# Last token group of a ConvFFN: 16 of 22 blocks of the down-projection by seven products for eight, their weight sums made in DRAM by accumulating DMAs

## The chip, the cores and the metric

One NeuronCore of one Trainium2 chip runs the program. The metric is the device time of one execution in microseconds (us); three runs of the kernel before gave 2209.5, 2211.93 and 2210.5 us, a median of 2210.5 us. Durations and waits come from one further execution that the hardware profiler recorded.

## The reference

One layer of a hybrid encoder on 2112 tokens (2048 of a prompt, 64 of a sample), in float32. An attention-like mixer comes first and is not touched by the change. What follows it, per token, with 1024 channels and 2816 hidden units:

```python
h2 = rmsnorm(x, g2) * (1 + sc2) + sh2
up = h2 @ w_up                                   # 1024 -> 2 * 2816
upp = concat([conv_buf, up], 1)                  # two earlier rows
conv = b_conv + sum(w_conv[j] * upp[:, j:j + T] for j in range(3))
a, g = split(conv, 2, -1)
x = x + gt2 * ((silu(g) * a) @ w_down)           # 2816 -> 1024
y = rmsnorm(x, g_final)
```

The outputs are y and the states that a next step needs.

## The kernel before

Channels lie on the 128 partitions and tokens along the free axis. The mixer fills about the first 800 us. The ConvFFN then runs in three token groups of FT = 704 tokens, from 800 to 1262, 1262 to 1727.6 and 1727.6 to 2205.6 us. A group is worked in two halves of FH = 352 tokens, which fit a PSUM bank. The third group holds the prompt's last 640 tokens and the 64 of the sample, so many of its vector operations are cut in two, at 640 of 704 or at 288 of 352.

**fp32 in three passes.** Each operand of a matmul is split into a rounded high part (ACT, `activation` with Copy) and the rest (DVE, a subtraction). A product is high x high, high x low and low x high: three matmuls for each 128x128 weight block and each half of the tokens (`PASSES`).

**Up-projection by seven products.** Hidden units come in 22 blocks of 128; for each block f a `Pair` computes the block of a and the block of g together. Four products of a half of the channels with a half of the tokens for each output, eight in all, are replaced by seven, in Strassen's manner, with sums of weights (`WS1` to `WS4`) and sums of tokens (B21, T2, T3 and so on). `product()` issues 12 matmuls of 352 columns each (L1522), so 84 for a pair. The sums of the weights lie in DRAM as `wsum`. Of the four, WS2 and WS1 are split in group 0 and stored to DRAM as split tiles (`wsplit`, 512 KB, `keep`, L374), which groups 1 and 2 load whole; WS3 and WS4 are loaded unsplit (256 KB) and split again in every group.

**Pair by pair.** While PE runs the products of one pair, DVE and ACT finish the pair before: sums of products into the extended tiles ea and eg (L1530, L1574), the convolution (scale on ACT L1505, taps on DVE L1510), silu (ACT L1616), the gate (DVE L1620) and the split of the result into `av` tiles (ACT L1637, DVE L1645).

**Down-projection.** The 22 blocks of a group are worked in four parts, `PARTS = ((0, 5), (5, 10), (10, 16), (16, 22))`: the pairs of a part, and then their share of the down-projection, whose contraction runs over the blocks of the part. Each of 8 output rows n takes nf blocks x 3 passes x 2 halves of matmuls (L1785) into two PSUM banks; `down_end` (L1800) then adds gt2 times the bank to the x tile of that row. The first NE = 3 rows are begun before the part's last blocks are ready. In the last part of the last group, rows 3 to 7 run in two sections of 448 and 256 tokens (`ENDS`), so that the final norm and the stores of the first section run under the second one; the weights of these rows stay in SBUF.

**Weights.** All weights are one list (`stream`) in the order in which PE needs them. `pump()` issues loads on SP's queue ahead of their use, into 4 raw tiles (RB, L350) or straight into one of 6 split tiles (WB; whole L355, to be split in place L358), and has ACT (L366) and DVE (L369) split them up to three units ahead. The order of instructions on PE, ACT, DVE and POOL is the order of the code (`manual_schedule`); side work (the next group's normalisation and its data sums, loads, the norm of the group before) is cut into steps, which `tick` and `do` place between the products.

## Time and profile before

| | |
|---|---|
| three runs | 2209.5, 2211.93, 2210.5 us (median 2210.5) |
| the profiled execution: span from the first to the last instruction | 2205.6 us |
| median of the runs less that span | 4.9 us |
| mixer | 0 to about 800 us |
| ConvFFN group 0, 1, 2 | 462, 465.6, 478 us |

A row of the table of windows gives the window, its length, then for PE, PE's weight loads (PEld), DVE, ACT and POOL the busy time and the number of instructions, then PE's granted clock (1.00 is full), the busy share of the DMA engines and the GB/s moved. A row of a group of instructions gives the source line, the engine, the operation, output <- inputs with partitions x elements, the number, and then busy time, mean ns of one, and how long the engine idled just before them and on whom it waited. A row of the page's list of DMA issues ends in the median time from issue to landing. All times are microseconds unless a row says otherwise.

### The profile page before, as it was taken

The page shows a single profiled execution, that of the slowest core. Times are in us where ns is not written, and L with a number is a line of the kernel's source. Part 1 is how long each engine was busy: PE and PEld are TensorE (multiplying, and loading weights), DVE is VectorE, ACT ScalarE, POOL GpSimd, SP SyncE. Part 2 cuts the span into 40 slices and gives each one's busy share as a digit, 9 for nine tenths or more (in the row PEclk, how much of TensorE's full clock was granted, in tenths as well). Part 3 has the DMA queues.
Part 4 walks back from the last instruction along what each step waited for, and adds up shares of the span by engine and source line. Part 5 has one row for each costly group of instructions (what it writes and reads, how often), then busy time and mean ns, then how long its engine had stood idle before and what let it go on. Part 6 is the DMA issues. An engine that isn't in the chain of part 4 may idle for free. (4 is left out here: it accounts for less than half of the span.)

```text
span 2205.6 us, 38165 instructions
## 1 busy us (share of the span) xinstructions
PE 2186.1 (99%) x13804; PEld 2079.2 (94%) x13804; DVE 1568.5 (71%) x2916; ACT 1005.3 (46%) x1993; POOL 203.0 (9%) x481
## 2 busy tenths in 40 slices
PE   8999999999999999999999999999999999999998
PEld 7888888888899999999999999999999999999998
DVE  5887669577765778787958587767667685767474
ACT  4653334235243455554636354545344443445354
POOL 0010000001000100010000210000001210101012
PEclk9999999999999999999999999999999999999999
DMA  9977987997898695767557876565458565353442
GB/s 355 367 242 264 333 275 243 324 324 239 292 323 272 223 310 177 234 205 239 188 173 233 266 245 200 183 214 175 144 169 285 186 190 166 111 173 121 150 148 81
DMA packets 279357, 498.58 MB, mean 226 GB/s; under 512 B 25176, under 2 KB 105432, under 8 KB 279168
## 3 DMA queue, kind: packets, MB, share of 16 engines
q1 hardware_dynamic: 267392, 468.05, 65.0%
q10 hardware_dynamic: 11776, 28.09, 3.4%
q8 instruction: 109, 1.79, 0.3%
q14 instruction: 80, 0.66, 0.1%
HBM read 385.29 MB, written 110.75 MB: 225 GB/s over the span
## 5 line engine op out<-in xcount | busy, mean ns | idle before, releaser
L1522 PE MATMUL mm<-hx,wt 128*128 128x352 f32 x5544 | 885.4, 321 | 1.0 <-DVE ea L1574 0.9
L1522 PEld LDWEIGHTS mm<-hx,wt 128*128 128x128 f32 x5544 | 879.5, 188 | 2.1 <-ACT wt L366 1.5
L1785 PE MATMUL mm<-av,wt 128*128 128x352 f32 (+2 forms) x3168 | 508.6, 321 | 0.4 <-DVE av L1645 0.3
L1785 PEld LDWEIGHTS mm<-av,wt 128*128 128x128 f32 x3168 | 502.6, 188 | 3.0 <-DVE av L1645 0.9
L423 PE MATMUL mm<-hl,wt 128*128 128x512 f32 (+2 forms) x1920 | 395.8, 358 | 1.7 <-DMA wt<-hl_kept 1.7
L366 ACT ACTIVATE wt<-raw 128x512 fp32r<-128x512 f32 (+3 forms) x494 | 274.5, 571 | 249.6 <-PE mm L1785 109.3
L369 DVE TENSOR_TENSOR wt<-raw,wt 128x512 fp32r<-128x512 f32 (+3 forms) x494 | 307.0, 637 | 87.5 <-ACT wt L366 81.4
L423 PEld LDWEIGHTS mm<-hl,wt 128*128 128x128 f32 x1920 | 312.6, 188 | 49.4 <-issue 5.3
L1800 DVE SCALAR_TENSOR_TENSOR x<-mm,MOD,x 128x352 f32<-128x352 f32 (+4 forms) x224 | 106.5, 526 | 128.8 <-PE mm L1785 128.8
L423 PE MATMUL mm<-mx,wt 128*128 128x512 f32 (+1 forms) x960 | 186.8, 353 | 0.0
L423 PEld LDWEIGHTS mm<-mx,wt 128*128 128x128 f32 x960 | 158.8, 188 | 25.4 <-ACT mx L1378 1.1
L1510 DVE SCALAR_TENSOR_TENSOR tg<-eg,V,tg 128x704 f32<-128x704 f32 (+1 forms) x132 | 125.7, 952 | 49.3 <-ACT tg L1505 46.8
L369 DVE TENSOR_TENSOR wt<-wt 128x512 fp32r<-128x512 f32 x176 | 121.8, 692 | 49.4 <-ACT wt L366 49.2
L366 ACT ACTIVATE wt<-wt 128x512 fp32r<-128x512 f32 x176 | 110.2, 626 | 75.1 <-DMA wt<-wsum 62.5
L1510 DVE SCALAR_TENSOR_TENSOR ta<-ea,V,ta 128x704 f32<-128x704 f32 (+1 forms) x132 | 125.6, 952 | 7.8 <-ACT ta L1505 5.4
L1645 DVE TENSOR_TENSOR av<-tg,av 128x704 fp32r<-128x704 f32 (+4 forms) x112 | 62.0, 588 | 43.2 <-ACT av L1637 43.0
L1570 ACT ACTIVATE u<-mm 128x352 f32<-128x352 f32 x66 | 30.6, 464 | 120.3 <-PE mm L1522 81.8
L1616 ACT ACTIVATE tg<-tg 128x704 f32<-128x704 f32 (+1 forms) x66 | 52.3, 793 | 68.9 <-DVE tg L1510 68.9
L203 DVE SCALAR_TENSOR_TENSOR acc<-raw,CA,acc 128x512 f32<-128x512 f32 x84 | 60.5, 744 | 32.1 <-DMA raw<-w_ada 32.1
L1530 DVE TENSOR_TENSOR eg<-mm,u 128x352 f32<-128x352 f32 x154 | 70.1, 467 | 18.4 <-ACT u L1585 11.2
L1114 PE MATMUL mm<-wt,hl 128*128 128x256 f32 (+1 forms) x576 | 70.9, 282 | 0.0
L1114 PEld LDWEIGHTS mm<-wt,hl 128*128 128x128 f32 x576 | 69.3, 188 | 1.0 <-issue 0.6
(299 smaller groups left out, 1951.9 us busy)
## 6 DMA issues: line engine op xcount, KB each, us to landing
wt<-hl_kept SPq DMA_DIRECT2D x108, 512.0 KB, 5.9
raw<-w_up SPq DMA_DIRECT2D x198, 256.0 KB, 3.1
wt<-wsum SPq DMA_DIRECT2D x176, 256.0 KB, 4.0
wt<-wsplit SPq DMA_DIRECT2D x88, 512.0 KB, 3.9
raw<-w_down SPq DMA_DIRECT2D x96, 256.0 KB, 3.9
w<-w_up SPq DMA_DIRECT2D x88, 256.0 KB, 5.4
wsum<-w SPq DMA_DIRECT2D x44, 512.0 KB, 5.7
wsplit<-wt SPq DMA_DIRECT2D x44, 512.0 KB, 5.0
```

The lines of the kernel that those rows point to most:

```text
L203: dve.scalar_tensor_tensor(out=acc[s], in0=w, scalar=CA[:, k, s:s + 1], in1=acc[s], op0=ALU.mult, op1=ALU.add)
L366: act.activation(u.w[:, 0, :u.n], u.raw[:, :u.n], AF.Copy)
L369: dve.tensor_tensor(out=u.w[:, 1, :u.n], in0=u.raw[:, :u.n], in1=u.w[:, 0, :u.n].bitcast(F32), op=ALU.subtract)
L423: pe.matmul(ps[bi][:, :hi - lo], U[:, a, k % 4 * P:(k % 4 + 1) * P], mv[k][:, b, lo:hi], start=(at == 0 and pi == 0), stop=(k == order[-1] ...
L1114: pe.matmul(ps[ti][:n, :cols], h[4 * kh + k4][:, b, lo:lo + n], U[:, a, k4 % 2 * cols:(k4 % 2 + 1) * cols], start=(kh == 0 and k4 == 0 and ...
L1510: dve.scalar_tensor_tensor(out=t[:, :E], in0=ext[:, j:j + E], scalar=wc(j, f), in1=t[:, :E], op0=ALU.mult, op1=ALU.add)
L1522: pe.matmul(ps[:, :FH], U[:, a, kc * P:(kc + 1) * P], Bo.at(nm, kc, b), start=(first and kc == 0 and pi == 0), stop=(kc == 3 and pi == 2), ...
L1530: dve.tensor_tensor(out=ext[:, d:d + b - a], in0=ps[:, a:b], in1=u[:, a:b], op=ALU.add)
L1616: act.activation(self.tg[:, :E], self.tg[:, :E], AF.Silu)
L1645: dve.tensor_tensor(out=cut(1), in0=self.of_tg(cut(0), a, b), in1=cut(0).bitcast(F32), op=ALU.subtract)
L1785: pe.matmul(ps[i][:, :hi - lo], U[:, a, k % 4 * P:(k % 4 + 1) * P], av[k](b, lo, hi), start=(k == 0 and (a, b) == PASSES[0]), stop=(k == n ...
L1800: dve.scalar_tensor_tensor(out=x3[n][:, a:b], in0=ps[i][:, a - lo:b - lo], scalar=gt2(n, s), in1=x3[n][:, a:b], op0=ALU.mult, op1=ALU.add)
```

## The change

**What it does in the last group** (`SGS = (2,)`). The parts become `SPARTS = ((0, 6), (6, 10), (10, 14), (14, 18), (18, 22))`. After each of the first four, `quad_down` does the down-projection of four blocks (two quads of two blocks each), 16 blocks in all. It takes the 8 output rows as four pairs m, and for each m seven products of two hidden blocks with half of the tokens, each over two quads: 7 x 2 x 3 = 42 matmuls of 352 columns (L1793), where eight would be 48. Products are added in PSUM where they can be; what remains goes to tiles `Y[m]` (a pair of x tiles) by ACT copies in the first stage and by DVE additions straight from PSUM in the others (L1805, L1811, L1818). The last pair of a part is held over: its last up-product runs inside `quad_down` (`midway`), its gate and the sums at the head of the next part. The last `down` takes blocks 16 to 21 as before (nf = 6).

**Sums of data.** The class `Quad` takes the place of `split_hi` and `split_lo` for blocks 0 to 15: the gate writes a fscr tile (L1697, cut at 640), and DVE and ACT make T1 to T4 and the splits of B11, B21, B22 and T1 to T4 from two of them.

**Sums of weights.** `down_sums` makes the four sums of w_down in DRAM (`dsum`), from the new input `w_quad` (the same weights in another order, arranged on the host): 16 copies of 512 KB on SP's queue and 16 DMAs on POOL's queue that add into DRAM. It moves by one step per pair, from group 0's first pair on (32 steps: group 0 and ten pairs of group 1).

**Weights of the last group.** For each m the stream has w_down 512 columns wide, two loads of 512 columns out of `dsum` (two runs of 1 KB per partition), and w_quad 256 columns wide. Also, group 1 stores the split tiles of WS3 and WS4 (`late_split`, 44 stores of 512 KB on SP), and group 2 loads them whole in place of loading and splitting the sums.

**End.** `from_quads` loads x for two rows into fscr tiles at a time, forms y1 - y3 and y2 + y3, and writes x3 = gt2 * Y + x (L1835 to L1840); `down_end` asks for it before it uses a row. x tiles are now allocated in pairs.

```diff
 PARTS = ((0, 5), (5, 10), (10, 16), (16, 22))
+SGS = (2,)
+SPARTS = ((0, 6), (6, 10), (10, 14), (14, 18), (18, 22))
...
     def sum_unit(g, f, i):
-        if i not in KEPT:
-            return (wsum[f, :, i], 512, INSIDE, None)
-        kept = wsplit[f, KEPT.index(i)]
-        return (kept, 512, WHOLE, None) if g else (wsum[f, :, i], 512, INSIDE, kept)
+        kept, first = (wsplit[f, KEPT.index(i)], 0) if i in KEPT else (late_split[f, (WS3, WS4).index(i)], 1)
+        if g > first:
+            return (kept, 512, WHOLE, None)
+        return (wsum[f, :, i], 512, INSIDE, kept if g == first else None)
+    def quad_units(m, j):
+        c = slice(j * 256, j * 256 + 256)
+        return [(w_down[2 * m, :, j * 512:(j + 1) * 512], 512), (dsum[m][:, S3D:S1D + 1, c], 512),
+                (dsum[m][:, S2D:S4D + 1, c], 512), (w_quad[3, m, :, c], 256)]
...
+    def down_sums():
+        for s, stages in ((S1D, (2, 3)), (S3D, (0, 2))):
+            for m in range(4):
+                tc.keep_in_program_order(nc.sync.dma_start(out=dsum[m][:, s], in_=w_quad[stages[0], m]))
+                yield
+            for m in range(4):
+                pool.dma_start(out=dsum[m][:, s], in_=w_quad[stages[1], m], accum_op=ALU.add)
+                yield
+        for s, base, q in ((S2D, S1D, 0), (S4D, S2D, 1)):
...
+    def quad_down(o, j, two, Y, first, midway):
+        for m in range(4):
...
+            def into(i, ps):
+                if first:
+                    act.activation(y[i], ps, AF.Copy)
+                else:
+                    dve.tensor_tensor(out=y[i], in0=ps, in1=y[i], op=ALU.add)
+            product(a, 0, 0, "B11", True)
+            act.activation(d, a, AF.Copy, scale=-1.0)
+            product(b, 1, 0, "T3", True)
+            into(3, b)
+            product(c, 1, 1, "T1", True)
+            dve.tensor_tensor(out=y[3], in0=y[3], in1=c, op=ALU.subtract)
+            if m == 0:
+                midway()
+            product(a, 0, 1, "B21", False)
+            into(0, a)
+            product(d, 2, 0, "T2", False)
+            dve.tensor_tensor(out=y[3], in0=d, in1=y[3], op=ALU.add)
+            product(b, 2, 1, "B22", False)
+            into(1, b)
+            product(c, 3, 0, "T4", False)
+            into(2, c)
+    def from_quads(o, Y, x3, made):
+        for m in range(4):
+            for n in (2 * m, 2 * m + 1):
+                st.append(fscr())
+                tc.keep_in_program_order(nc.sync.dma_start(out=st[-1], in_=x2d[n, :, o.t0:o.t0 + FT]))
+            yield
+            dve.tensor_tensor(out=y[1], in0=y[1], in1=y[3], op=ALU.subtract)
+            dve.tensor_tensor(out=y[2], in0=y[2], in1=y[3], op=ALU.add)
+            yield
+            for i, n in enumerate((2 * m, 2 * m + 1)):
+                for (a, b, s) in o.segs:
+                    dve.scalar_tensor_tensor(out=x3[n][:, a:b], in0=x3[n][:, a:b], scalar=gt2(n, s),
+                                             in1=st[i][:, a:b], op0=ALU.mult, op1=ALU.add)
+                made.append(n)
+                yield
...
             def down_end(n, ps, secs):
+                while Y and n not in made:
+                    next(conv)
```

**Where instructions move.** On PE in the last group, before, from the second part's pairs on: the pairs' products (L1522) and then the plain down-projection (L1785). A row is a run of equal instructions with its number.

```order
L1522 MATMUL mm<-hx,wt 128x352 x408
L1785 MATMUL mm<-av,wt 128x352 x18
L1522 MATMUL mm<-hx,wt 128x352 x12
L1785 MATMUL mm<-av,wt 128x352 x222
L1522 MATMUL mm<-hx,wt 128x352 x492
```

After, at the second part of the same group: fewer pairs, and the first row pair of a quad stage (b is the tile of B11, av the other data sums).

```order
L1543 MATMUL mm<-hx,wt 128x352 x324
L1793 MATMUL mm<-b_20248,wt 128x352 x3
L1793 MATMUL mm<-b_20508,wt 128x352 x3
L1793 MATMUL mm<-av,wt 128x352 x12
L1543 MATMUL mm<-hx,wt 128x352 x12
L1793 MATMUL mm<-av,wt 128x352 x24
```

The held pair's last product (12) now stands after 18 of 42 quad products, and three more rounds of 42 follow.

On DVE in a plain row of the last group, before (x is the row's x tile, wt <- raw a weight split):

```order
L369 TENSOR_TENSOR wt<-raw,wt 128x512
L1800 SCALAR_TENSOR_TENSOR x_19511<-mm,MOD,x_19511 128x352
L1800 SCALAR_TENSOR_TENSOR x_19511<-mm,MOD,x_19511 128x288
L1800 SCALAR_TENSOR_TENSOR x_19511<-mm,MOD,x_19511 128x64
L369 TENSOR_TENSOR wt<-raw,wt 128x512
```

After, on DVE in one row pair of a quad stage (x is the tile Y[m]):

```order
L1805 TENSOR_TENSOR x_19878<-mm,x_19878 128x352
L1811 TENSOR_TENSOR x_19878<-x_19878,mm 128x352
L1805 TENSOR_TENSOR x_19878<-mm,x_19878 128x352
L390 TENSOR_TENSOR wt<-raw,wt 128x512
L1818 TENSOR_TENSOR x_19878<-mm,x_19878 128x352
L1805 TENSOR_TENSOR x_19878<-mm,x_19878 128x352
L390 TENSOR_TENSOR wt<-raw,wt 128x512
L1805 TENSOR_TENSOR x_19878<-mm,x_19878 128x352
L390 TENSOR_TENSOR wt<-raw,wt 128x256
L390 TENSOR_TENSOR wt<-raw,wt 128x512
```

Three operations and one or two splits for a row have become six additions and four splits for two rows.

On DVE in the last part's down-projection, before, two early rows, and the first of the sectioned ones:

```order
L1800 SCALAR_TENSOR_TENSOR x_19511<-mm,MOD,x_19511 128x352
L1800 SCALAR_TENSOR_TENSOR x_19511<-mm,MOD,x_19511 128x288
L1800 SCALAR_TENSOR_TENSOR x_19511<-mm,MOD,x_19511 128x64
L1800 SCALAR_TENSOR_TENSOR x_19513<-mm,MOD,x_19513 128x352
L1800 SCALAR_TENSOR_TENSOR x_19513<-mm,MOD,x_19513 128x288
L1800 SCALAR_TENSOR_TENSOR x_19513<-mm,MOD,x_19513 128x64
L369 TENSOR_TENSOR wt<-raw,wt 128x256
L369 TENSOR_TENSOR wt<-raw,wt 128x512
L1800 SCALAR_TENSOR_TENSOR x_19670<-mm,MOD,x_19670 128x448
L369 TENSOR_TENSOR wt<-raw,wt 128x256
```

After, the same place: the end of the quad sums stands ahead of the rows that need it.

```order
L1835 TENSOR_TENSOR x_19878<-x_19878 128x352
L1836 TENSOR_TENSOR x_19878<-x_19878 128x352
L1840 SCALAR_TENSOR_TENSOR x_19878<-x_19878,MOD,fscr 128x640
L1840 SCALAR_TENSOR_TENSOR x_19878<-x_19878,MOD,fscr 128x64
L2058 SCALAR_TENSOR_TENSOR x_19878<-mm,MOD,x_19878 128x352
L2058 SCALAR_TENSOR_TENSOR x_19878<-mm,MOD,x_19878 128x288
L2058 SCALAR_TENSOR_TENSOR x_19878<-mm,MOD,x_19878 128x64
L390 TENSOR_TENSOR wt<-raw,wt 128x256
L1840 SCALAR_TENSOR_TENSOR x_19878<-x_19878,MOD,fscr 128x640
L1840 SCALAR_TENSOR_TENSOR x_19878<-x_19878,MOD,fscr 128x64
L390 TENSOR_TENSOR wt<-raw,wt 128x512
L1835 TENSOR_TENSOR x_19879<-x_19879 128x352
```

Four operations for every row pair are new there, and each row's first operation on its x tile waits for them.

More of the change, by code (lines that the diff above doesn't have):

```diff
@@ L109, in drain @@
     def drain(*which):
-        for i in which or (0, 1, 2, 3, 4):
+        for i in which or (0, 1, 2, 3, 4, 5):
             while bg[i]:
@@ L1556, in rest, with extra @@
                         step(pair)
+            def extra(i):
+                for at, step in self.more:
+                    if at == i:
+                        step()
             rest((old, Pair.copy_u4), (older, Pair.gate))
@@ L1618, in gate @@
         def gate(self):
+            if self.quad:
+                self.quad.gate(self)
+                return
             E = EX - 2 if self.o.last else FT
@@ new lines, in down_sums @@
+    def down_sums():
[8 more added lines that the diff above has]
+            for m in range(4):
+                tc.keep_in_program_order(nc.sync.dma_start(out=dsum[m][:, s], in_=dsum[m][:, base]))
+                yield
+            for m in range(4):
+                pool.dma_start(out=dsum[m][:, s], in_=w_quad[q, m], accum_op=ALU.add)
+                yield
@@ L1752, in tile_layer @@
     x3, ssum = [], None
+    bg[5].append(down_sums())
     for o in fgroups:
         Bo = B[o.g]
[L1755 to L1757 removed]
+        quads, more, held = {}, [], []
+        Y = None
+        for pi, (f0, f1_) in enumerate(SPARTS if o.g in SGS else PARTS):
+            lastp = f1_ == NF
+            if o.g in SGS and lastp:
+                av = [None] * (NF - PARTS[-1][0])
+            nf = f1_ - (PARTS[-1][0] if o.g in SGS and lastp else f0)
@@ L1769, in tile_layer, with midway @@
                 drain(0)
+            if o.g in SGS and pi == 0:
+                Y = [f2.tile([P, 2 * FT], F32, tag=f"x{2 * m}", name=f"x{2 * m}") for m in range(4)]
+                x3 = [Y[n // 2][:, n % 2 * FT:(n % 2 + 1) * FT] for n in range(KD)]
+            if o.g in SGS and not lastp:
+                old = pair.before
+                pair.copy_u4()
+                for (_, step) in last_lows:
+                    step()
+                todo.extend([both_of(pair.sum_g1, old.gate), pair.sum_a, pair.scale_a])
+                def midway():
+                    do(9)
+                    pair.last_product()
+                    todo.append(both_of(pair.sum_g0, pair.scale_g))
+                quad_down(o, pi, [quads[2 * pi], quads[2 * pi + 1]], Y, pi == 0, midway)
+                do(9)
+                held.append(pair)
+                continue
+            if o.g in SGS:
+                made = []
+                conv = from_quads(o, Y, x3, made)
+                bg[1].append(conv)
             if pi == 0 and o.g > 0:
```

154 lines of the change are left out of this document (143 added, 11 removed).

## The prediction

> **What bounds the kernel now.** I read the page's busy shares first, then the table of windows by token group, then the waits and the timeline of PE, then DVE's groups in the last group.
>
> ```profile
> PE 2186.1 (99%) x13804; PEld 2079.2 (94%) x13804; DVE 1568.5 (71%) x2916; ACT 1005.3 (46%) x1993; POOL 203.0 (9%) x481
> ```
>
> ```profile
> 800.00:1262.00 462.00, 462.00 (x2922) 461.37 (x2921) 349.58 (x565) 241.83 (x423) 43.35 (x95) 1.00 0.68 221
> 1262.00:1727.60 465.60, 464.39 (x2927) 463.33 (x2925) 333.71 (x546) 219.18 (x390) 40.10 (x97) 1.00 0.62 199
> 1727.60:2205.60 478.00, 469.32 (x2958) 466.13 (x2956) 317.85 (x609) 210.41 (x395) 67.75 (x195) 0.99 0.47 147
> 2143.40:2184.60 41.20, 41.20 (x241) 39.87 (x240) 23.00 (x45) 21.97 (x40) 8.60 (x10) 1.00 0.22 61
> ```
>
> PE is busy throughout a group at full clock; the third group's 8.7 us without PE (478.00 - 469.32) are mostly the tail after the last matmul. A busy PE need not be at its peak, so I ask what a matmul costs when nothing holds it up. PE's timeline in the last group lists runs of equal matmuls with their start, length and number:
>
> ```profile
> 1835.38 64.79 PE L1522 MATMUL mm<-hx,wt 128*128 128x352 f32 x408
> ...
> 1904.78 35.34 PE L1785 MATMUL mm<-av,wt 128*128 128x352 f32 x222
> 1939.95 78.10 PE L1522 MATMUL mm<-hx,wt 128*128 128x352 f32 x492
> ```
>
> By the order, 408 + 18 + 12 = 438 matmuls lie between the first and the second quoted start, and 222 between the second and the third. (1904.78 - 1835.38) / 438 = 0.1584 us and (1939.95 - 1904.78) / 222 = 0.1584 us. Both projections run at one cadence, without stalls: the kernel is bound by the number of matmuls, and one of 352 columns is worth 0.158 us.
>
> **The change part by part.**
>
> *Products.* The first three parts' 16 blocks cost 16 x 8 rows x 3 passes x 2 halves = 768 matmuls; the new stages cost 4 stages x 4 row pairs x 42 = 672, as the order shows them. 96 x 0.1584 = **-15.2 us**. All of it is on the path, if DVE, ACT and DMA keep up with a PE that asks for more of them. That is the rest of the question.
>
> *DVE beside the pairs.* The rows of the last group:
>
> ```profile
> L369 DVE TENSOR_TENSOR wt<-raw,wt 128x512 fp32r<-128x512 f32 x96 | 64.6, 690 | 26.5 <-ACT wt L366 26.5
> L369 DVE TENSOR_TENSOR wt<-wt 128x512 fp32r<-128x512 f32 x44 | 30.8, 699 | 11.3 <-ACT wt L366 11.3
> L1620 DVE TENSOR_TENSOR tg<-ta,tg 128x706 f32<-128x706 f32 x22 | 19.6, 889 | 2.8 <-ACT tg L1616 2.8
> L1800 DVE SCALAR_TENSOR_TENSOR x<-mm,MOD,x 128x352 f32<-128x352 f32 x29 | 16.8, 581 | 51.7 <-PE mm L1785 51.6
> L1800 DVE SCALAR_TENSOR_TENSOR x<-mm,MOD,x 128x288 f32<-128x288 f32 x27 | 13.7, 507 | 0.0
> L1530 DVE TENSOR_TENSOR eg<-mm,u 128x352 f32<-128x352 f32 x22 | 11.4, 520 | 0.4 <-PE mm L1522 0.3
> L1800 DVE SCALAR_TENSOR_TENSOR x<-mm,MOD,x 128x64 f32<-128x64 f32 x32 | 8.8, 275 | 0.0
> L1645 DVE TENSOR_TENSOR av<-tg,av 128x352 fp32r<-128x352 f32 x16 | 8.4, 524 | 10.1 <-ACT av L1637 9.9
> L1645 DVE TENSOR_TENSOR av<-tg,av 128x288 fp32r<-128x288 f32 x16 | 7.2, 452 | 0.0
> L369 DVE TENSOR_TENSOR wt<-raw,wt 128x256 fp32r<-128x256 f32 x16 | 6.7, 417 | 2.1 <-ACT wt L366 2.1
> L1645 DVE TENSOR_TENSOR av<-tg,av 128x640 fp32r<-128x640 f32 x6 | 5.0, 830 | 5.9 <-ACT av L1637 5.9
> L1645 DVE TENSOR_TENSOR av<-tg,av 128x64 fp32r<-128x64 f32 x22 | 4.8, 219 | 0.0
> L1800 DVE SCALAR_TENSOR_TENSOR x<-mm,MOD,x 128x448 f32<-128x448 f32 x5 | 3.4, 679 | 4.7 <-PE mm L1785 4.7
> ```
>
> A pair loses two splits of sums (2 x 0.699), three of data (0.524 + 0.452 + 0.219) and the gate (0.889): 3.48 us. It gains the cut gate (0.830 + 0.219, by the split of the same widths) and half of a quad's sums and splits, (5 x 0.520 + 3 x 0.889) / 2 = 2.63: 3.68 us. That is even, and 84 x 0.1584 = 13.3 us of PE hide it. Price: nothing; with the cover gone, 16 pairs x 0.2 = 3 us.
>
> *DVE in a quad stage.* A row pair has six additions of 352 columns and four splits: 6 x 0.520 + 3 x 0.690 + 0.417 = 5.6 us under 42 x 0.1584 = 6.65 us of PE. The additions read PSUM, as L1530 does, so 0.520 is a like row. The first row pair also hosts the held pair's last product (12 more matmuls, 8.55 us) with its gate, about 3 us. That fits by a hair. The raw tiles: a row pair of loads comes round all 4 raw tiles once, and a tile is held from its issue over the landing to its split. Two rows of the last group bear on that, the view of the raw loads of L350 from 1800 to 2140 and ACT's row for the high parts:
>
> ```profile
> DMA to landing us min/median/max: 1.8/2.9/5.0
> ```
>
> ```profile
> L366 ACT ACTIVATE wt<-raw 128x512 fp32r<-128x512 f32 x96 | 57.7, 622 | 58.8 <-PE mm L1785 42.9 <-PE mm L1522 6.9 <-DMA raw<-w_down 6.4
> ```
>
> With the median landing, the high part and the low part, 2.9 + 0.62 + 0.69, and an estimated 1.4 for the issue and for the queues on ACT and DVE, the cycle is 5.6 us, below 6.65. I take **+1 us** for the stages; the bounds are 0 and the price of the third rival.
>
> *Last part.* The end of the quad sums is new on DVE: eight additions of 352 columns between SBUF tiles and eight cut STT with fscr. Like rows stand in the groups of the last two token groups:
>
> ```profile
> L701 DVE SCALAR_TENSOR_TENSOR fscr<-fscr,G,rbn 128x640 f32<-128x640 f32 x8 | 7.0, 878 | 0.1
> ...
> L701 DVE SCALAR_TENSOR_TENSOR fscr<-fscr,G,rbn 128x64 f32<-128x64 f32 x8 | 2.2, 277 | 0.0
> L754 DVE TENSOR_TENSOR fscr<-fscr 128x352 f32<-128x352 f32 x4 | 2.1, 519 | 0.0
> ```
>
> 8 x 0.519 + 8 x (0.878 + 0.277) = 13.4 us. The window 2143.40 to 2184.60 held 23.00 us of DVE in 41.20, so 36.4 fit in sum, at 88%. But they crowd between the ends of row 0 and row 7: three rows of (0.581 + 0.507 + 0.275), the 13.4, and four rows of an addition and two splits (0.679 + 0.690 + 0.417), 24.6 us, while PE takes 18 x 0.1584 for the early rows' last blocks and 18 matmuls of 448 columns, 18 x 0.1584 x 448 / 352 = 3.63, for each of four rows: 17.4 us. Splits run up to three units ahead, so some 5 of the 7.2 us of them fall earlier; the x loads must land first. The view of DMA issues has a row for the same kind of load:
>
> ```profile
> fscr<-x2d SPq DMA_DIRECT2D x16, 352.0 KB, 5.9
> ```
>
> A first load that isn't early enough costs a part of that 5.9. I take **+3 us**; bounds 0 (PE's free banks absorb the lag) and 24.6 - 17.4 = 7.
>
> *Group 1's stores.* 44 stores of split tiles are new on SP's queue. Group 0 made the same number of the same size, and shows what they cost beside a full PE: nothing (462.00 of 462.00).
>
> ```profile
> wsplit<-wt SPq DMA_DIRECT2D x44, 512.0 KB, 5.0
> ```
>
> But the start of group 1 is its densest place, for DVE and for the DMA engines:
>
> ```profile
> 1275.00:1288.00 13.00, 13.00 (x84) 13.00 (x83) 10.28 (x18) 6.18 (x11) 1.12 (x4) 1.00 0.70 220
> 1288.00:1302.00 14.00, 13.12 (x84) 12.87 (x83) 13.85 (x23) 8.02 (x14) 2.52 (x4) 1.00 0.69 238
> 1302.00:1315.00 13.00, 13.00 (x83) 12.90 (x83) 12.93 (x23) 6.63 (x13) 2.56 (x3) 1.00 0.84 294
> 1315.00:1328.00 13.00, 13.00 (x83) 13.00 (x83) 10.28 (x16) 7.93 (x14) 0.98 (x4) 1.00 0.71 244
> ```
>
> DVE has 13.85 busy of 14 there, and a late weight would find no slack. A store holds its split tile for some 5.0 us more, one of six. **+1 us**, bounds 0 and 7 (first rival).
>
> *Sums of weights.* POOL's 16 accumulating DMAs stand, in order, before its copy into eg. POOL idles there:
>
> ```profile
> POOL eg L1488 <- DVE tg L1510: 83.8, 21, 5.1
> ```
>
> 83.8 / 21 = 4.0 us at a time, so an issue is covered. The sums are read only in the last group, 300 us on. Nothing; if POOL were held over a whole 5.0-us transfer and PE behind it, 16 x (5.0 - 4.0) = 16 us. Such a DMA is in no trace of before; the 5.0 of a plain store of the same size is the nearest row. The 16 copies on SP's queue stand ahead of weight loads that are issued a few units early: nothing, in group 0 likewise.
>
> Sum: -15.2 + 1 + 3 + 1 = -10.2. The profiled span of 2205.6 becomes 2195.4; 4.9 us lie around it (2210.5 - 2205.6), so **2200.3 us**.
>
> **The rivals.**
>
> *First: DMA saturates at the start of group 1.* The four windows moved (220 x 13 + 238 x 14 + 294 x 13 + 244 x 13) / 53 = 249 GB/s. The stores add 2 x 524288 B in 13.3 us = 79, the sums a 512 KB step per pair, 39 (79, if reading and writing DRAM both count): 367 to 407 GB/s. The highest window of the trace is
>
> ```profile
> 55.00:110.00 55.00, 53.98 (x279) 45.09 (x278) 46.31 (x90) 33.41 (x78) 2.46 (x2) 1.00 1.01 367
> ```
>
> So 53 x (407 / 367 - 1) = 5.8 us at worst, which takes the place of the 1: 2200.3 + 4.8 = **2205**. For it: DVE has no slack there. Against: weights are loaded ahead, and the demand may be just 367. The Trainium skill ("DMA: Bandwidth & Descriptors", Specifications) gives a limit of about 358 GB/s of HBM for one core; by it the estimate is 53 x (407 / 358 - 1) = 7.3 us. This trace's 367 lies above that figure, so the measurement decides.
>
> *Second: DVE becomes the bound of the last group.* Each of four stages loses 2 us (the first row pair "by a hair"), the last part 6, group 1 the 1: 8 + 6 + 1 - 15.2 = 0, **2210**, no change. For it: DVE's 88% in the last part. Against: the group's DVE falls elsewhere, by 30.8 us of L369 on wt.
>
> *Third, slower: the ring of raw tiles starves the quad stages.* Two of three wide loads in a row pair take 1-KB runs out of dsum. The page's only loads in such runs land late:
>
> ```profile
> w<-w_up SPq DMA_DIRECT2D x88, 256.0 KB, 5.4
> ```
>
> With 5.4 for 2.9 the cycle of 5.6 becomes 8.1 us against 6.65, for 16 row pairs (8.1 - 6.65) x 16 = 23; PE then waits and DVE's order puts additions behind the late split: -15.2 + 23 + 4 (the last part and group 1) = +12, **2222**. The gain is gone at (15.2 - 4) / 16 = 0.7 us a row pair, a cycle of 7.35 us or a landing of about 4.65. For it: four raw tiles only, and 3.5 wide units for two rows. Against: those 5.4 were measured in the mixer with the DMA engines near full; the last group moves 147 GB/s.
>
> *Fourth: POOL is held by the accumulating DMAs.* 16 us by the bound above: about **2216**.
>
> That the change doesn't do what it says (fewer matmuls) the order excludes.
>
> **How the numbers follow.** Forecast 0.76; first rival 0.09; second 0.08; third 0.05; fourth 0.02. Least: -15.2 with the terms near their lower bounds, 2195.3; I leave 2194.5 for the tail. The forecast's own range reaches to about 2205, with the last part at its bound of 7 and half a microsecond more; the first rival lies at its rim. To take in the better part of the second, I go to 2208. About 0.2% (4.4 us) is what a measurement of this kernel can tell from no change. Faster by over that: the forecast, the first rival in most of its cases, 0.83; within: the second and the rest of the first, 0.10; slower: the third, the fourth, 0.07.
>
> **What would show it.** Group 2 shorter by about 11 us (478.0 to 467), group 1 465.6 to at most 467, group 0 unchanged at 462. Quad stages at 0.158 us for each matmul, no row of PE waiting on L1805 to L1818 for more than 1 us in all, and DVE near 85% there. In the last part DVE at 85 to 90% and PE's waits on L1840 or on x2 of 1 to 4 us. It is wrong where group 1 grows by more than 3 us (first), where quad stages take over 0.17 us a matmul with PE waiting for raw<-dsum (third) or for DVE (second), or where POOL's rows before eg show waits on DMA issue (fourth).

## The result and the profile after

The changed kernel took 2228.45 us (median of 4 runs, 2227.81 to 2230.27) where the kernel before took 2210.0 us (4 runs beside them, 2208.49 to 2211.93): a ratio of 1.0083, 95% interval 1.0071 to 1.0095. It is slower by some 18 us, where 10 us faster was forecast.

The profiled execution had a span of 2228.5 us (its time was 2230.27), 22.9 more than the span before. The windows of the three token groups (the columns are those of the first such table) say where:

```profile
805.00:1277.60 472.60, 466.58 (x2923) 462.35 (x2922) 350.30 (x566) 240.79 (x424) 47.77 (x105) 1.00 0.76 241
1277.60:1754.30 476.70, 466.06 (x2925) 463.43 (x2925) 333.98 (x546) 219.11 (x389) 45.27 (x103) 1.00 0.78 255
1754.30:2228.50 474.20, 462.75 (x2862) 458.28 (x2860) 351.83 (x645) 219.41 (x382) 75.16 (x195) 0.99 0.58 185
```

Group 0 grew from 462.0 to 472.6 us and group 1 from 465.6 to 476.7; the change does nothing there but make sums and store split weights, and PE now idles 6.0 and 10.6 us in them (length less PE busy); the other 4.6 us of group 0 stand inside PE's busy time (466.58, before 462.00), as longer distances between the starts of matmuls, around the stops and in stretches of a longer cadence (below). Group 2, in which the products are saved, shrank by 3.8 us only. The remaining 5.0 us lie ahead of the FFN: group 0 starts at 805.0, not 800.0. That is scatter: over the profiles of this study the start lay between 799.5 and 805.7 us whatever was changed behind it.

In groups 0 and 1 the waits of ACT changed most. Group 0 before:

```profile
ACT wt L366 <- DMA wt<-wsum: 39.5, 35, 4.1
```

and after:

```profile
ACT wt L387 <- DMA wt<-wsum: 57.9, 44, 4.4
```

(total, times, longest). ACT waits for weights that land late; DVE and PE follow. The views of DMA issues in group 0 show the same in the landing times of the weight loads, before and after:

```profile
raw<-w_up SPq DMA_DIRECT2D x66, 256.0 KB, 4.0
```

```profile
raw<-w_up SPq DMA_DIRECT2D x66, 256.0 KB, 5.6
```

One stall can be followed through. POOL issues an adding DMA; the DMA engines are full while it moves (share 1.03, at 236 GB/s only); ACT waits 4.42 us for a weight sum; PE, seven microseconds on, has no operand for 1.47 us. Rows of POOL, of the windows, of ACT and of PE in the changed kernel:

```profile
945.44 0.83 POOL L1771 DMA_DIRECT2D dsum<-w_quad  x1 [0.31 <-issue]
```

```profile
947.00:954.00 7.00, 6.72 (x42) 6.43 (x42) 6.34 (x11) 3.67 (x7) 0.32 (x1) 1.00 1.03 236
```

```profile
955.67 0.63 ACT L387 ACTIVATE wt<-wt 128x512 fp32r<-128x512 f32 x1 [4.42 <-DMA wt<-wsum]
```

```profile
962.47 17.38 PE L1543 MATMUL mm<-hx,wt 128*128 128x352 f32 x108 [1.47 <-DVE ea L1604]
```

So the adding DMA doesn't block POOL (its issue took 0.83 us); it takes the DMA engines away from the loads. Whether bytes ran out in this window isn't shown. The engines were full at 236 GB/s, where the busiest stretch of the kernel before moved 367 over 55 us. But of the window's 236 x 7.00 = 1652 KB, 512 KiB (524 KB) are the adding DMA's and are counted once; counted three times (source read, old sum read, new sum written) they give an estimate of (1652 + 2 x 524) / 7.00 = 386 GB/s. The Trainium skill ("DMA: Bandwidth & Descriptors", Specifications) puts the limit of one core at about 358 GB/s of HBM. This case's 367 GB/s lie above that, so it settles nothing here.

Group 2 has two losses of another kind. PE's timeline in the first quad stage (start, length of the run, number):

```profile
1839.11 3.96 PE L1793 MATMUL mm<-av,wt 128*128 128x352 f32 x24
1842.91 1.13 PE L1793 MATMUL mm<-b,wt 128*128 128x352 f32 x6
1843.89 6.16 PE L1793 MATMUL mm<-av,wt 128*128 128x352 f32 x36
1849.89 1.13 PE L1793 MATMUL mm<-b,wt 128*128 128x352 f32 x6
1850.85 6.16 PE L1793 MATMUL mm<-av,wt 128*128 128x352 f32 x36
```

The first row pair's 24 take (1842.91 - 1839.11) / 24 = 0.1583 us each, the known cadence. From the second row pair on it is (1849.89 - 1843.89) / 36 = 0.1667 us, at full granted clock and without a wait. The trace of single matmuls shows four such long-cadence stretches, one for each stage, of 191 or 192 matmuls (126 of the stage, the rest in the pair behind it): 767 x 0.0083 = 6.4 us at most, since the six of B11 at the head of a row pair are quicker ((1850.85 - 1849.89) / 6 = 0.160 us in the third). The other loss is the last part: from its first down-projection row to the end of the span 2228.5 - 2159.84 = 68.7 us, before 2205.6 - 2143.37 = 62.2. PE's timeline there, and the wait of DVE that starts it:

```profile
2179.64 6.75 PE L2041 MATMUL mm<-av,wt 128*128 128x448 f32 x32 [0.20 <-DVE x L2058]
2187.11 1.07 PE L2041 MATMUL mm<-av,wt 128*128 128x448 f32 x4 [0.72 <-DVE wt L390]
2189.04 0.67 PE L2041 MATMUL mm<-av,wt 128*128 128x448 f32 x2 [0.86 <-ACT wt L387]
2190.14 9.19 PE L2041 MATMUL mm<-av,wt 128*128 128x448 f32 x36 [0.43 <-DVE wt L390]
```

```profile
DVE x L1840 <- DMA fscr<-x2d: 2.8, 1, 2.8
```

### The profile page after: what moved, and what is told of

It is laid out like the page before. It is cut to its first block, busy times and chain, and to the rows that moved or that the text cites. A ratio compares the mean times of both kernels' runs of the same rounds, so it can differ in the third digit from the quotient of the medians.

```text
span 2228.5 us, 38266 instructions
## 1 busy us (share of the span) xinstructions
PE 2187.7 (98%) x13708; PEld 2073.8 (93%) x13708; DVE 1603.4 (72%) x2952; ACT 1013.1 (45%) x1979; POOL 220.0 (10%) x497
## 5 line engine op out<-in xcount | busy, mean ns | idle before, releaser
L1543 PE MATMUL mm<-hx,wt 128*128 128x352 f32 x5544 | 893.0, 322 | 13.4 <-DVE ea L1604 6.9
L2041 PE MATMUL mm<-av,wt 128*128 128x352 f32 (+2 forms) x2400 | 389.0, 322 | 5.8 <-ACT av L1676 2.5
L387 ACT ACTIVATE wt<-raw 128x512 fp32r<-128x512 f32 (+3 forms) x510 | 288.7, 579 | 231.9 <-PE mm L2041 60.0
L2041 PEld LDWEIGHTS mm<-av,wt 128*128 128x128 f32 x2400 | 381.5, 188 | 10.7 <-ACT av L1676 3.1
L390 DVE TENSOR_TENSOR wt<-raw,wt 128x512 fp32r<-128x512 f32 (+3 forms) x510 | 321.9, 645 | 77.8 <-ACT wt L387 76.1
L390 DVE TENSOR_TENSOR wt<-wt 128x512 fp32r<-128x512 f32 x132 | 91.2, 691 | 59.3 <-ACT wt L387 58.7
L2058 DVE SCALAR_TENSOR_TENSOR x<-mm,MOD,x 128x352 f32<-128x352 f32 (+4 forms) x152 | 77.9, 558 | 76.3 <-PE mm L2041 76.3
L387 ACT ACTIVATE wt<-wt 128x512 fp32r<-128x512 f32 x132 | 82.8, 629 | 108.1 <-DMA wt<-wsum 90.4
L1793 PE MATMUL mm<-av,wt 128*128 128x352 f32 x576 | 98.0, 326 | 0.0
L1793 PEld LDWEIGHTS mm<-av,wt 128*128 128x128 f32 x576 | 95.3, 188 | 0.0
L1551 DVE TENSOR_TENSOR eg<-mm,u 128x352 f32<-128x352 f32 x154 | 70.0, 466 | 22.9 <-ACT u L1619 12.2
```

The source lines that it names most:

```text
L387: act.activation(u.w[:, 0, :u.n], u.raw[:, :u.n], AF.Copy)
L390: dve.tensor_tensor(out=u.w[:, 1, :u.n], in0=u.raw[:, :u.n], in1=u.w[:, 0, :u.n].bitcast(F32), op=ALU.subtract)
L1543: pe.matmul(ps[:, :FH], U[:, a, kc * P:(kc + 1) * P], Bo.at(nm, kc, b), start=(first and kc == 0 and pi == 0), stop=(kc == 3 and pi == 2), ...
L1551: dve.tensor_tensor(out=ext[:, d:d + b - a], in0=ps[:, a:b], in1=u[:, a:b], op=ALU.add)
L1793: pe.matmul(ps, U[:, x, w:w + P], quad.d[nm][:, z], start=(start and k == 0 and pi == 0), stop=(k == 1 and pi == 2), skip_group_check=not ...
L2041: pe.matmul(ps[i][:, :hi - lo], U[:, a, k % 4 * P:(k % 4 + 1) * P], av[k](b, lo, hi), start=(k == 0 and (a, b) == PASSES[0]), stop=(k == n ...
```

## The experiments

**Are the sums the cost, and which of their DMAs?** Four kernels take the 32 DMAs apart. The first leaves them all out.

```diff
-    dsum = dr.tile([4, P, 4, NP * P], F32, tag="dsum", name="dsum")
...
-    bg[5].append(down_sums())
...
+    arrays["dsum"] = arrays["w_quad"].transpose(1, 2, 0, 3)
```

> Left out: the 32 DMAs that make the weight sums in DRAM; the quads read an array of unsummed weights in the same layout, so the last group's work is the same. Theory S (these DMAs cost what groups 0 and 1 lost): group 0 back to 462 to 464 us from 472.6, group 1 to 468 to 471 from 476.7, time about 2212. Rival L (the late stores of split tiles and SP's queue are the cost, the sums only a bystander): group 0 gains 2 us at most, group 1 stays at 475 to 477, time about 2226.

Measured: 2205.87 us, ratio 0.9987 (0.9978 to 0.9997). Groups 0, 1 and 2:

```profile
800.90:1262.90 462.00, 462.00 (x2922) 461.39 (x2921) 349.21 (x565) 242.39 (x424) 42.31 (x95) 1.00 0.68 221
1262.90:1730.30 467.40, 464.26 (x2926) 462.78 (x2925) 334.11 (x546) 218.94 (x389) 40.86 (x97) 1.00 0.75 248
1730.30:2203.90 473.60, 461.03 (x2862) 456.58 (x2860) 352.08 (x645) 219.35 (x382) 74.87 (x195) 0.99 0.59 186
```

Group 0 is back at 462.0, with PE busy throughout, and group 1 at 467.4: 10.6 and 9.3 us are the sums'. Theory S holds. What is left in group 1, 1.8 us over before, I put down to the late stores. Even so the kernel gains only 0.1%.

The second lets POOL's DMAs copy in place of adding.

```diff
-                pool.dma_start(out=dsum[m][:, s], in_=w_quad[stages[1], m], accum_op=ALU.add)
+                pool.dma_start(out=dsum[m][:, s], in_=w_quad[stages[1], m])
...
-                pool.dma_start(out=dsum[m][:, s], in_=w_quad[q, m], accum_op=ALU.add)
+                pool.dma_start(out=dsum[m][:, s], in_=w_quad[q, m])
```

> The 16 DMAs on POOL's queue copy in place of adding (the sums are left out, the DMAs stay). If the adding is the cost (each such DMA holds the DMA engines about 2.4 times as long as a plain one): group 0 at 465 to 467, group 1 at 471 to 474, time about 2218. If any DMA of 512 KB there costs the same: no change, 2227 to 2229. If POOL's queue is the cost: no change either.

Measured: 2215.53 us, ratio 1.003 (1.0018 to 1.0042); groups 465.6 and 471.9. Adding alone is worth 472.6 - 465.6 = 7.0 and 476.7 - 471.9 = 4.8 us. POOL's queue on the page, adding and copying (packets, MB, share of 16 engines):

```profile
q0 software_dynamic: 2304, 8.39, 2.5%
```

```profile
q0 software_dynamic: 2304, 8.39, 1.4%
```

2.5% of 2228.5 us over 16 DMAs is 3.5 us of all 16 engines for each 512 KB; 1.4% of 2213.8 is 1.9 us. The same bytes took these engines nearly twice the time when they were added (1.8 times, where 2.4 was expected).

The third leaves POOL's DMAs out and keeps SP's copies.

```diff
-                pool.dma_start(out=dsum[m][:, s], in_=w_quad[stages[1], m], accum_op=ALU.add)
...
-                pool.dma_start(out=dsum[m][:, s], in_=w_quad[q, m], accum_op=ALU.add)
```

> The 16 DMAs on POOL's queue are left out, the 16 copies on SP's queue stay (sums are wrong). With the plain copies on both queues the groups took 465.5 and 471.9 us, without any 462.0 and 467.4. If volume is what costs: half of that, 463 to 464 and 469 to 470, time about 2210. If the copies cost by blocking SP's queue: all of it, 465 and 472, time 2214 to 2216. If they are free there: 462 and 467.5.

Measured: 2214.04 us, ratio 1.0018 (1.0009 to 1.0028); groups 465.8 and 471.8. By the numbers that were set, this is "all of it": 16 copies on SP's queue cost as much as they and 16 copies on POOL's. So volume alone isn't the price, and the place in SP's queue may be. The fourth moves the copies to POOL's queue.

```diff
-                tc.keep_in_program_order(nc.sync.dma_start(out=dsum[m][:, s], in_=w_quad[stages[0], m]))
+                pool.dma_start(out=dsum[m][:, s], in_=w_quad[stages[0], m])
...
```

> The 16 copies of the sums are issued on POOL's queue, in the same steps, in place of SP's. Copies alone on SP's queue had cost 3.8 us in group 0 and 4.4 in group 1, plain copies on POOL's queue beside them nothing. If the place in SP's queue, ahead of weight loads, is the cost of the copies: group 0 at about 469 (462 + 7 for the adding), group 1 at 472, time 2220. If the volume is: no change, 472.6 and 476.7, 2226 to 2229.

Measured: 2223.07 us, ratio 1.0046 (1.0029 to 1.0063); groups 472.2 and 475.6 against 472.6 and 476.7. The two measures disagree. The groups hardly moved, but the execution that was profiled was the longest of the four (2227.0 us); the median lies 5.4 us below the changed kernel's, between the two expectations, and the two intervals do not overlap. So the queue isn't the main cost, but a part of some 5 us isn't excluded; the combinations below bear on it again.

**Does the place in time matter?** The steps go from the pairs to the down-projections, where the DMA engines had the most room: in the changed kernel a share of 0.49 to 0.67 in the first three of each group, though 0.89 and 0.90 in the last.

```diff
             extra(5)
-            tick(5)
...
             def down_end(n, ps, secs):
+                if n % 2:
+                    tick(5)
```

> The 32 steps of the weight sums are moved from the pairs to the down-projections of groups 0 and 1, four to each, where the DMA engines were busy for about half of the time. Theory S with contention (the sums delay the loads of the pairs, whose part of the DMA engines is full): most of the 20 us comes back, group 0 at 462 to 466, group 1 at 467 to 472, time 2206 to 2213. If each sum costs PE time wherever it stands: 2225 to 2229.

Measured: 2224.97 us, ratio 1.0069 (1.0053 to 1.0086); groups 471.1 and 475.6. Almost nothing came back, but the stalls moved: with sums in the pairs they lay all over a part, here most of them within 13 us behind a down-projection's end. I put that down to the last of the four steps and moved the steps up by some rows, in the two combinations below (rows 1, 3, 4, 5). In the first of them group 0 was 466.8 and group 1 471.1, in the second 468.9 and 476.5, and the stalls still stood there. POOL's timeline in that first combination shows what a place in the code is worth on an engine with nothing else to do:

```profile
978.12 2.59 POOL L1781 DMA_DIRECT2D dsum<-w_quad  x3 [0.18 <-issue]
984.42 0.81 POOL L1781 DMA_DIRECT2D dsum<-w_quad  x1 [3.71 <-ACT tg L1649]
```

The down-projection ran from 973.9 to 1013.9; its four DMAs, which the code spreads over it, all went out within 7 us, from 978.12 to 985.23. From 974 to 996 the loads beside them landed in 10 us, where those of the kernel before took 3.5 in the like stretch (view of DMA issues, first this kernel, then before):

```profile
raw<-w_down SPq DMA_DIRECT2D x4, 256.0 KB, 9.8
```

```profile
raw<-w_down SPq DMA_DIRECT2D x5, 256.0 KB, 3.5
```

The plain down-projection rode that out. As I read it, the next group's side work fell behind, and the loads for the next pairs then came due together with it; no run tests that alone. What the trace shows is that ACT waited for wsum from 1014.5 to 1019.8, and that PE stopped for 3.01 us up to 1020.84.

**Bursts or volume?** That left two readings: some 5 us at a time in which no weights come, or the volume of the adding DMAs. The sums go into quarters of 32 partitions, three to a pair, so that POOL's copies of UC stand between them and pace them.

```diff
...
+                for r in range(0, P, 32):
+                    pool.dma_start(out=dsum[m][r:r + 32, s], in_=get(m)[r:r + 32], **kw)
+                    yield
...
             extra(0)
+            tick(5)
...
             extra(1)
+            tick(5)
```

This kernel also has the early end and the offset of the T2 and T4 tiles, below.

> The sums in 128 DMAs of 128 KB (32 partitions each) in place of 32 of 512 KB, all on POOL's queue, three to a pair in groups 0 and 1; with the early end and the offset of T2 and T4 (group 2 was 462.4 us with these two). If bursts of 5 us are the cost: group 0 at 462 to 465, group 1 at 467 to 470, time 2197 to 2204. If the volume of the adding DMAs is: 470 to 473 and 474 to 477, time 2211 to 2216.

Measured: 2202.41 us, ratio 0.9964 (0.9951 to 0.9976), the first kernel of the study with a clear gain. Its groups and POOL's queue:

```profile
804.40:1266.90 462.50, 462.50 (x2921) 461.33 (x2921) 349.20 (x565) 241.18 (x423) 85.91 (x159) 1.00 0.77 239
1266.90:1737.00 470.10, 465.45 (x2927) 463.31 (x2926) 334.41 (x546) 219.23 (x389) 82.75 (x159) 1.00 0.82 264
1737.00:2199.40 462.40, 453.59 (x2861) 451.35 (x2860) 347.23 (x645) 219.31 (x382) 73.61 (x195) 0.99 0.60 190
```

```profile
q0 software_dynamic: 6144, 16.79, 3.9%
```

PE doesn't stop in group 0: 462.50 busy of 462.50, at nearly the DMA share and GB/s of the changed kernel (0.77 against 0.76, 239 against 241). Three quarters of 512 KB go out for a pair, where it was 512 KB, so group 0 carries less of the sums. By GB/s times length it moved 110.5 MB, the changed kernel 113.9 and the one without sums 102.1: the sums' share is 8.4 MB for 11.8. A cost in proportion to volume would still be 10.6 x 8.4 / 11.8 = 7.5 us. It was 0.5 us here and 2.3 in the kernel without late stores below (464.3), whose sums are the same. So in group 0 it was bursts, not volume. Against the kernel with all sums on POOL's queue, the size, the rate and the pacing of the DMAs changed together; how much each of them counts isn't shown. In group 1, where the stores come on top, 2.7 us remain over the 467.4 without sums.

**Late stores.** They were undone alone, and again with the small pieces.

```diff
...
-        kept, first = (wsplit[f, KEPT.index(i)], 0) if i in KEPT else (late_split[f, (WS3, WS4).index(i)], 1)
+        if i not in KEPT:
+            return (wsum[f, :, i], 512, INSIDE, None)
+        kept = wsplit[f, KEPT.index(i)]
...
```

> Only the late stores undone: WS3 and WS4 are split again in group 2. Theory S: group 0 unchanged at 472, group 1 gains 2 to 5 us (from 476.7), group 2 loses some of it to 44 more splits on DVE and ACT; time 2224 to 2229. Rival L: group 1 back to 466 to 468, time about 2218 or less.

Measured: 2221.93 us, ratio 1.0056 (1.004 to 1.0072); groups 471.7, 466.9, 477.3. Group 0 is theory S's, group 1 is rival L's, and the time lies between them: neither had the two acting together. Group 1 comes back wholly though the sums are in it, as it does with the stores but without the sums (467.4). Either alone costs 1 to 2 us there, both together 11. In group 2 the stores save 477.3 - 474.2 = 3.1 us.

> The same without the late stores (WS3 and WS4 split again in group 2). Late stores without sums had cost group 1 1.8 us, sums without late stores 1.2, both together 11. If the pieces cure the collision: group 1 466, group 2 465 to 466, time within 2 us of the run with late stores. If the collision stays there: group 1 5 us or more below the run with late stores, and 2 us or more faster in all.

Measured: 2204.81 us, ratio 0.9969 (0.9959 to 0.998); groups 464.3, 467.9, 466.3. Group 1 gains 2.2 us, group 2 gives back 3.9; the two kernels are 2.4 us apart, their intervals overlap, and the collision is mostly gone with the pieces.

**The longer cadence of matmuls.** First the quads' tiles: the low parts' second half is moved by 16 bytes, as the kernel before does in some av tiles and in T1 (`NUDGE`).

```diff
-            d = f2.tile([P, XT], F32R, tag="av", name="av", bufs=6).rearrange("p (a h t) -> p a h t", a=2, h=2)
+            t = f2.tile([P, XT], F32R, tag="av", name="av", bufs=6)
+            hi = t[:, :2 * XR].rearrange("p (h t) -> p h t", h=2)[:, :, :FH]
+            lo = t[:, 2 * XR:4 * XR - 2 * NUDGE].rearrange("p (h t) -> p h t", h=2)[:, :, :FH]
...
```

> The low parts of the quads' data tiles are moved so that the second half of each lies 16 bytes off its former place; nothing else. Theory C (a run of matmuls at 0.1667 in place of 0.1584 us starts where all operands keep the same alignment, and the offset that the kernel before has in its av and T1 tiles ends it): the four runs of 192 slow matmuls behind each quad stage's first row pair are gone, group 2 shortens by 5 to 6.4 us, time about 2222. Rival D (the slower matmuls come from DMA or DVE traffic beside them): the runs stay, time unchanged at 2228.

Measured: 2225.7 us, ratio 1.0079 (1.0057 to 1.0101), not to be told from the changed kernel by its time. The trace shows more: group 2 went from 474.2 to 471.6, the pairs behind a stage from 51.9 to 51.3, and in each stage the long-cadence stretch is now cut into pieces of 36, 25, 25 and 25. Within a row pair they begin after the product with the moved T3 tile and end in the one with the moved B22. So the offset switches the cadence, both ways: layout, not traffic, and theory C is right on the cause and was wrong that any offset ends it.

The second gave B11's tile the layout of the others.

```diff
...
-            t = spare[0].tile([P, FT], F32R, tag=("rbn", "ssum")[self.p % 2], name="b11")
-            self.d["B11"] = self.halves(t)
+            t = spare[0].tile([P, 2 * XR], F32R, tag=("rbn", "ssum")[self.p % 2], name="b11")
+            self.d["B11"] = self.halves(t)[:, :, :FH]
```

> The tile of B11 gets the layout of the av tiles: its high and low parts 1536 bytes apart, not 1408. If the odd distance starts the slow runs of matmuls: no run of 192 at 0.1667 us is left, quad stages take 28.5 us (180 x 0.1584) and not 29.5, pairs after them 51.3 and not 51.9, group 2 6 us shorter, time about 2222. If seven products with many operands make them: no change.

Measured: 2229.64 us, ratio 1.0086 (1.0071 to 1.0101). A miss: three of the four long-cadence stretches grew to 246. B11's odd distance doesn't start them. The third test goes to the kernel before.

```diff
-NUDGE, NUDGED = 4, "T1"
+NUDGE, NUDGED = 0, "T1"
```

> The kernel before with the 16-byte offset of its av and T1 tiles taken out. If equal alignments let slow runs of matmuls (0.1667 in place of 0.1584 us) go on: runs of hundreds of slow matmuls in all groups, tens of us longer. If the slow runs belong to the seven products of the quads: no change, 2210.

Measured: 2249.28 us, one run, against 2209.85. PE's timeline in group 1:

```profile
1338.90 37.16 PE L1785 MATMUL mm<-av,wt 128*128 128x352 f32 x222
1375.90 68.16 PE L1522 MATMUL mm<-hx,wt 128*128 128x352 f32 x408
1443.90 3.16 PE L1785 MATMUL mm<-av,wt 128*128 128x352 f32 x18
```

(1443.90 - 1375.90) / 408 = 0.1667 us where before it was 0.1584, again without a wait. Group 0 stayed at 461.7 us, against the expectation, so a missing offset alone doesn't start the longer cadence. Groups 1 and 2 took 485.3 and 497.6 us: the trace of single matmuls has one stretch of 2547 matmuls in it from 1330 us on, and after some 30 us in the known cadence at the head of group 2 a second of 2388. The longer cadence has nothing to do with the quads as such.

**The end.** The end of the quad sums goes into the last part's pairs, four steps to a pair.

```diff
+            if o.g in SGS and lastp:
+                made = []
+                conv = from_quads(o, Y, x3, made)
+                bg[1].append(conv)
             for f in range(f0, f1_):
...
+                if o.g in SGS and lastp:
+                    steps += [(at, lambda: tick(1)) for at in (1, 3, 5)]
...
-            if o.g in SGS:
-                made = []
-                conv = from_quads(o, Y, x3, made)
-                bg[1].append(conv)
```

> The changed kernel with the end of the quad sums (loads of x, the two additions, x3) moved from the last down-projection into the last part's four pairs, four steps to a pair. If it is this work that made the last part 5 to 6 us longer (68.7 us from its first row to the end, 62.2 before): 62 to 64 us, time 2222 to 2224. Rival: the last part is longer because of its weights (a ring that starts empty after the pairs): it stays at 67 to 69.

Measured: 2221.26 us, ratio 1.005 (1.0035 to 1.0065). The last part took 2218.7 - 2155.60 = 63.1 us for 68.7, and its rows are one run again, as before the change:

```profile
2155.60 4.04 PE L2043 MATMUL mm<-av,wt 128*128 128x352 f32 x24
2159.48 2.15 PE L1543 MATMUL mm<-hx,wt 128*128 128x352 f32 x12
2161.47 35.57 PE L2043 MATMUL mm<-av,wt 128*128 128x352 f32 x204
```

**Combinations.** Two kernels have the early end, the sums at rows 1, 3, 4 and 5, and each another offset; the first has all sums on POOL's queue and moves only the tile of B21 and B22, the second leaves the copies on SP's and moves only that of T2 and T4.

```diff
+                if n in (1, 3, 4, 5):
+                    tick(5)
...
+            off = 2 * NUDGE if names == ("T2", "T4") else 0
+            lo = t[:, 2 * XR:4 * XR - off].rearrange("p (h t) -> p h t", h=2)[:, :, :FH]
```

> Combination: the end of the quad sums in the last part's pairs; all 32 DMAs of the sums on POOL's queue, one each behind rows 1, 3, 4 and 5 of the down-projections of groups 0 and 1; of the quads' tiles only that of B21 and B22 has its second low part moved by 16 bytes. With the sums at rows 1, 3, 5 and 7 the stalls stood 0.5 to 13 us behind the end of a down-projection, so with the last one some 10 us earlier they should go: groups 462 to 464 and 467 to 469, group 2 468.6 less 0 to 6 for the slow matmuls: time 2198 to 2206. If each adding DMA costs wherever it is: 2210 to 2216.

Measured: 2209.28 us, ratio 0.9994 (0.9985 to 1.0004). Groups 466.8, 471.1, 465.2: the sums as told above; half of the long matmuls are left (two runs of 39 in each stage). Of its two expectations the time is nearest to "each adding DMA costs wherever it is".

> The same with the 16 copies on SP's queue, and of the quads' tiles only that of T2 and T4 moved by 16 bytes. If SP's queue costs: 2 to 5 us above the other; if only the place in time matters, the same groups 0 and 1. The slow runs: if a moved operand that closes a row pair brings the fast pattern back, 0 to 4 us of the 6.4 are left.

Measured: 2211.47 us, ratio 1.0006 (0.9997 to 1.0016). Groups 468.9, 476.5, 462.4. Its time is 2.2 us longer with a group 2 that is 2.8 us shorter, so the copies on SP's queue cost some 5 us here (7.5 in the profiled groups 0 and 1), as expected for the case that the queue costs. That fits the 5.4 us between the medians above: the place in SP's queue is a part of the price, not most of it. With the moved T4 tile, which closes each row pair, no long-cadence stretch is left in the stages, and PE's timeline shows the cadence that the prediction had used, (1843.59 - 1837.87) / 36 = 0.1589 us:

```profile
1837.87 5.88 PE L1803 MATMUL mm<-av,wt 128*128 128x352 f32 x36
1843.59 1.12 PE L1803 MATMUL mm<-b,wt 128*128 128x352 f32 x6
```

Group 2 at 462.4 against 478.0 is 15.6 us saved: the 96 matmuls' worth, with the early end and without long-cadence stretches. It takes the late stores too: without them group 2 was 466.3, 11.7 us saved, where PE waits 2.6 us for DVE's L1604.

## Why the prediction was wrong

*The step that failed: "Sums of weights ... Nothing".* It asked whether POOL is held and whether the sums are ready in time, and both answers were right: an issue took 0.83 us, and nothing waited for dsum. It didn't ask what 32 transfers of 512 KB do to the loads that share the DMA engines with them. Measured: 2228.45 - 2205.87 = 22.6 us, more than the whole gain. In the spans of the groups it is 10.6 and 9.3 us, of which adding is 7.0 and 4.8. The copies on SP's queue, "nothing" too, cost 3.8 and 4.4 when they were alone. Its bound of 16 us came from a mechanism that isn't there (fourth rival: POOL held); the true price lay outside.

*The first rival* had the kind of mechanism, DMA engines that are full, but not its place and size. It compared averages over 53 us of group 1 in GB/s with the highest 367; the loss stood in group 0 as much, in a window of 236 GB/s, and came from stretches of some 5 us in which adding packets held the engines (3.3 to 8.3 us by the trace of single packets, at a DMA share of 0.99 to 1.07). In hindsight, the row that could have warned stood in the table of windows of before: group 0 at a DMA share of 0.68 on average leaves little room for a transfer that takes all engines for 3.5 us, with the weights split three units ahead.

*Products, -15.2 us:* the number of matmuls was right, their price wrong. "Both projections run at one cadence" had been read from two kinds of runs and was carried over to a third. Some 760 matmuls ran in the longer cadence, +6 us: with the early end group 2 took 468.6 us without the offset and 462.4 with that of T2 and T4. With the offset the gain is there.

*Last part, +3, bounds 0 to 7:* the mechanism was right, DVE's crowding and a wait for x (2.8 us); the size was 68.7 - 62.2 = 6.5, near the bound. With the end moved, 63.1 - 62.2 = 0.9 were left. (A row pair has six new operations on DVE, not four: two additions and two of L1840, each cut in two. The sum of 13.4 us had them all.) A stretch at half clock is in it: the granted clock from 2160 to 2206.7 was 0.96 on average.

```profile
2160.00:2206.70 46.70, 44.11 (x240) 40.58 (x240) 38.37 (x69) 22.23 (x40) 9.66 (x11) 0.96 0.37 115
```

DVE was busy 38.37 of 46.70, 82%, where 85 to 90 were foretold.

*Group 1's stores, +1:* alone 1.8, within the bounds; but the terms don't add. With the sums beside them the two cost 11.

*Pairs and quad stages:* right. No addition of a quad stage kept PE waiting, the raw ring held, and without long-cadence stretches a stage took 28.6 us for 180 x 0.1584 = 28.5. In the changed kernel DVE was busy 23.43 of 29.70 us of the second stage, 79%, where 85 were foretold. Of the second rival only its 6 us for the last part came, and the third did not occur: the loads out of dsum landed in a median 2.8 us.

```profile
raw<-dsum SPq DMA_DIRECT2D x32, 256.0 KB, 2.8
```

What stays open: why a 16-byte offset switches the cadence of matmuls and what starts the slow one; why an adding DMA keeps the engines longer; why 16 copies on SP's queue cost as much as they and 16 more on POOL's; and why stores and sums lose so much more together than each alone (the runs show that it is so, and that small pieces nearly cure it).

## What to carry to other kernels

Background transfers are priced in time of the DMA engines and by the longest stretch for which they hold them, set against how far ahead the loads of the critical stages run; averages of GB/s over a stage say little. Cut them small and let an instruction that is paced by the work stand between them: on an idle engine the order of the code sets no time. And before a saving of matmuls is counted, look whether the new operands keep the old ones' cadence.

## What was not expected of the hardware

- A DMA that adds into DRAM took 3.5 us of all 16 DMA engines for 512 KB, a copy on the same queue 1.9 us. Where the adding DMAs stood in the down-projections it was 2.9 us (2.1% of 2223.4 us over 16).
- Matmuls of 352 columns have two steady cadences, 0.1584 and 0.1667 us, at the same granted clock. A run stays in one over hundreds of matmuls; moved operands switch it. Taking out the kernel's two 16-byte offsets cost 2249.28 - 2209.85 = 39 us.
- After some stops of PE the granted clock was half of full for some 3.5 us. In the mixer of the changed kernel PE was busy 1.20 us of 3, and in the next 3.5 us the clock was 0.51 on average; in the first combination, with the stop of 3.01 us, it averaged 0.84 over 11 us. Not every stop had this: in the changed kernel the clock stayed at 1.00 from 1311 to 1315 us, behind a stop of 2.60 us.

```profile
668.00:671.00 3.00, 1.20 (x10) 1.01 (x9) 0.99 (x3) 0.38 (x1) 0.00 (x0) 1.00 1.01 332
671.00:674.50 3.50, 3.50 (x16) 3.50 (x17) 2.60 (x9) 2.06 (x9) 0.00 (x0) 0.51 0.91 333
```

```profile
1014.00:1025.00 11.00, 7.99 (x42) 7.71 (x41) 3.96 (x8) 2.28 (x5) 0.00 (x0) 0.84 0.92 325
```
